# First phase in a fixed order with batched modulation, and mixers with 32-column products gathered

## The chip, the cores and the metric

The kernel runs on one core of one Trainium2 chip. The metric is device time in microseconds, as the median of several runs. One further execution was profiled; times "at" some microsecond below count from the start of its span.

## The reference, cut to what matters

One layer (DEPTH 1) is applied to 256 prompt rows and to 8 single-row samples that carry a recurrent state. All products with weights are in float32 accuracy.

```python
mod = silu(c) @ w_ada + b_ada                  # 2048 x 12288, six parts
h = rmsnorm(x, g_pre_mix) * (1 + sc1) + sh1
z = h @ w_in                                   # 2048 x 15376
y_a = spatial gating of gelu(z_uv)             # branch A
y_b = HGRN2 recurrence, 8 heads, 128 x 128     # branch B, state S' = f S + k v^T
y_c = GLA recurrence, 4 heads, 128 x 256       # branch C, the same form
merged = sum over n of sigmoid(z_gate[n]) * (y_n @ w_branch[n])
x = x + gt1 * rmsnorm(merged @ w_out, g_post_mix)
x = x + gt2 * rmsnorm(relu(h2 @ w_mlp_up)**2 @ w_mlp_down, g_post_mlp)
```

Outputs are the rows of prompt and samples, the final states of both recurrences, and branch A's normalised v rows of the samples.

## The kernel before, in words

**Layout.** Features lie on partitions, 16 feature tiles of 128. The columns are the 256 prompt rows and the 8 samples, 264 in all. The weights are the stationary operand. Each weight block is split into two float32r parts (`split`: ACT casts the high part, L102, and DVE subtracts for the low part, L99), and so are the activations; a product of a 128x128 weight tile is three matmuls of 264 columns (L459, L460, L461 in `granule`). There are 13872 of these matmuls, and they are what the kernel is about.

**Stream of weights.** `plan` lists every block of weights in the order of use. `Stream` loads a block of 512 KB over SP (L419) three blocks ahead of its use and splits it two blocks ahead. A block feeds 24 matmuls and is called an item below. Raw blocks have 6 buffers (`raw`), the split halves 4 (`whi`, `wlo`), which is two items.

**Modulation.** `mod` is needed before `h`. Its products put the 9 conditioning vectors on 32 columns of the PE array, and four such products with their own column strip fill 128 columns (`ada_step`, L236; `ada_round`, L265). The trace shows two records for each of these float32 products. The shift and scale of the first sub-layer are computed by `ada_first` for two or four feature tiles at a time (CHUNKS 2, 2, 4, 4, 4), while the first phase multiplies the feature tiles that are already known with the first 5120 columns of w_in. `ada_round` computes the other parts later, one step of four products at a time.

**Stages.** After a start (x loaded, normed, transposed; first chunk of the modulation) come the first phase (1920 matmuls), the GLA columns (816), branch A with its gates (1152), the gate tiles of branch B (384), branch B (1152), gate tiles of C (384), branch C (1152), the output projection (768) and the MLP (6144). The stages from the GLA columns to branch C are called the mixers' stages here: beside their matmuls run, as generators, `mixer_a`, three `mixer_r` (two groups of HGRN2 heads, one of GLA heads) and, for each group, `samples_r`.

**Generators and queues.** `linear` calls `granule` and then lets three queues advance by fixed rates: `bg` (the mixers), `bs` (the samples), `ba` (rounds of the modulation). That fixes the program's order. The order on each engine is then decided by the framework's scheduler, which models the engines and transfers and may move an instruction ahead of others where its operands allow it.

**Samples.** `samples_r` makes 8 steps for each HGRN2 group and 16 for GLA. A step fetches 256 KB of state (`st`, 3 buffers, L777) and 256 KB of broadcast values (`vbc`, 2 buffers, L779, from a scratch in device memory), both over SP, two steps ahead in the program. ACT scales the state (L791), DVE adds (L793), Pool writes it back (L794), and PE reads it out on 32-column strips (L799). Buffer `st` is free for the next fetch only after that read-out.

**Small products on 32 columns.** Beside L236, L265 and L799 there are the levels of the recurrences' decay matrices: `small_level` (L852, 32 products of 32 columns) and the halves of 32 (L908, 16 products on 32 columns) and of 64 (L916, 8 products on 64 columns).

Of the kernel before, what the change touches and what calls it, by code (L numbers as in the profile page):

```python
# [35 lines left out]
RATES = ((1.7, 0.2, 0.3), (1.5, 0.35, 0.32), (1.5, 0.25, 0.28), (1.0, 0.05, 0.22))  # L36
ST_BUFS = 3
# [3 lines left out]
NQ = 28.0  # L41
R0 = 0.34
ADA_AHEAD = 1
# [3 lines left out]
FILL = (5.0, 9.0)  # L47


@with_exitstack  # L50
def hybrid_step_kernel(
# [53 lines left out]
    # ---------------------------------------------------------------- constants  # L105
    cst = const([P, 904], "cst")
    nc.sync.dma_start(cst, consts)
# [3 lines left out]
    nc.gpsimd.dma_start(msk, masks.rearrange("p (l t) -> p l t", l=6))  # L111

    # ---------------------------------------------------------------- small vectors
# [7 lines left out]
    # x: prompt rows as two token tiles, the samples' feature tiles as rows  # L121
# [8 lines left out]
    nc.sync.dma_start(st1[0:96, :], flat128(b_ada))  # L130
    nc.sync.dma_start(st1[96:112, :], flat128(g_pre_mix))
    nc.sync.dma_start(st1[112:128, :], flat128(g_post_mix))
# [3 lines left out]
    for v, n in rows2:  # L136
        nc.gpsimd.dma_start(st2[n2:n2 + n, :], flat128(v))
        n2 += n

# [7 lines left out]
    ps = sm()  # L147
    T.transpose(ps[:, 0:128], st1, ident)
    T.transpose(ps[:, 128:128 + n2], st2[0:n2, :], ident[0:n2, 0:n2])
    vec = const([P, 128 + n2], "vec")  # L150
    V.tensor_copy(vec, ps[:, 0:128 + n2])
    V.tensor_scalar(vec[:, 172:175], vec[:, 172:175], 0.5, None, ALU.mult)
# [22 lines left out]
    def sum_features(v, n, w):  # L175
        """Sums of v [P, n, w], which it overwrites, over its features (partitions and n tiles), on every partition."""
        while n > 1:
            n //= 2
            add(v[:, 0:n, :], v[:, 0:n, :], v[:, n:2 * n, :])
        ps = sm([P, w])  # L180
# [1115 lines left out]
```

## Time and profile before

| | us |
|---|---|
| runs, median of 3 (lowest to highest) | 2010.1 (2008.6 to 2014.9) |
| profiled execution, span | 2009.9 |
| PE busy / PE weight loads / DVE / ACT / POOL in that span | 1948.6 / 1814.9 / 1191.6 / 1002.0 / 40.5 |
| mean granted PE clock | 0.988 |
| HBM traffic over the span | 219 GB/s |

The profiled execution has no time of its own beside its span; the span stands 0.2 us below the median of the runs, and sums below are made against it. PE matmuls are pipelined, so that a mean duration of 288 ns does not mean one matmul each 288 ns: what counts is the pitch from start to start. A row of the timeline gives start, length, engine, line, operation, tiles and count; in brackets stands the idle time before it and what ended that. "x8" on a line of the modulation is eight records, that is, four products.

### The profile page before, as it was taken

The numbers are of one execution on the slowest core, as the hardware profiler recorded it, in microseconds if no ns is written. First come the engines' busy times: TensorE is split into PE (matmuls) and PEld (weight loads), VectorE is DVE, ScalarE is ACT, GpSimd is POOL, SyncE is SP. The second block draws the span as 40 slices with busy tenths as digits, with TensorE's granted clock in tenths as the row PEclk, the third lists the DMA queues.
The fourth block names the chain that finished last, engine by engine and source line by source line (L and its number), as shares of the span: only waits on it lengthen the run. The fifth ranks groups of instructions, "written<-read, shape, count | busy, mean of one in ns | idle before, by whom it ended". The sixth has DMA issues, their size and how long they took to land.

```text
span 2009.9 us, 42161 instructions
## 1 busy us (share of the span) xinstructions
PE 1948.6 (97%) x17020; PEld 1814.9 (90%) x17020; DVE 1191.6 (59%) x2105; ACT 1002.0 (50%) x1773; POOL 40.5 (2%) x66
## 2 busy tenths in 40 slices
PE   5999999999999999899899999999999999999997
PEld 4779898989988987789899995999999999999996
DVE  3456566777475687445555556555555555555656
ACT  4434354576664574454444445555444445454543
POOL 1000000000000000000000000000000000000000
PEclk9999999999999999999999999999999999999998
DMA  9887978787798668887555866655555555555552
GB/s 311 289 300 244 292 229 250 219 276 222 255 286 280 211 207 255 271 273 228 189 179 180 271 200 231 212 185 179 180 183 182 181 179 184 179 183 180 180 179 84
DMA packets 378179, 442.05 MB, mean 220 GB/s; under 512 B 14914, under 2 KB 339136, under 8 KB 377984
## 3 DMA queue, kind: packets, MB, share of 16 engines
q1 hardware_dynamic: 372592, 424.27, 66.7%
q0 software_dynamic: 4496, 13.90, 1.9%
q8 instruction: 133, 2.18, 0.4%
q10 hardware_dynamic: 896, 1.19, 0.2%
q14 instruction: 62, 0.51, 0.1%
HBM read 427.60 MB, written 11.70 MB: 219 GB/s over the span
## 4 chain that ended last, share of the span: by engine, by line
PE 91%; DMA 4%; DVE 2%; ACT 2%; issue 1%; SPq 0%; ACTq 0%; DVEq 0%
PE mm L459 28%; PE mm L460 27%; PE mm L461 27%; PE ada L265 3%; DMA st<-in_state_gla_dram 2%; PE ada L236 2%; DMA raw<-in_w_ada_dram 1%; PE sm L540 1%; PE sm L799 1%; DVE wlo L99 1%; ACT whi L102 1%; DMA raw<-in_w_in_dram 1%; PE sm L852 1%; DMA st<-in_state_hgrn_dram 0%; DMA b<-in_g_post_mix_dram 0%
## 5 line engine op out<-in xcount | busy, mean ns | idle before, releaser
L459 PE MATMUL mm<-b,whi 128*128 128x264 f32 x4624 | 1332.1, 288 | 17.3 <-ACT b L102 8.0
L460 PE MATMUL mm<-b,whi 128*128 128x264 f32 x4624 | 1321.9, 286 | 1.5 <-DVE b L99 1.5
L461 PE MATMUL mm<-b,wlo 128*128 128x264 f32 x4624 | 1317.3, 285 | 3.2 <-DVE wlo L99 3.2
L99 DVE TENSOR_TENSOR wlo<-raw,whi 128x512 fp32r<-128x512 f32 x1156 | 790.6, 690 | 654.1 <-ACT whi L102 616.3
L102 ACT CAST whi<-raw 128x512 fp32r<-128x512 f32 x1156 | 709.1, 619 | 799.5 <-PE mm L460 720.8
L459 PEld LDWEIGHTS mm<-b,whi 128*128 128x128 f32 x4624 | 873.4, 189 | 78.6 <-issue 31.4
L461 PEld LDWEIGHTS mm<-b,wlo 128*128 128x128 f32 x4624 | 872.8, 189 | 13.4 <-issue 7.2
L460 PEld LDWEIGHTS mm<-b,whi 128*128 128x128 f32 x4624 | 873.4, 189 | 11.4 <-issue 8.8
L96 DVE TENSOR_TENSOR b<-b,mm 128x528 f32<-128x528 f32 x136 | 94.9, 698 | 17.8 <-PE mm L461 17.7
L265 PE MATMUL ada<-raw,cT 128*32 128x512 f32 x464 | 75.6, 616 | 3.0 <-DMA raw<-in_w_ada_dram 3.0
L791 ACT ACTIVATE st<-st,fs 128x128 f32<-128x128 f32 (+1 forms) x96 | 37.0, 430 | 69.9 <-DMA st<-in_state_gla_dram 46.3
L793 DVE SCALAR_TENSOR_TENSOR st<-vbc,b,st 128x128 f32<-128x128 f32 (+1 forms) x96 | 33.9, 390 | 62.1 <-ACT st L791 49.0
L236 PE MATMUL ada<-raw,cT 128*32 128x256 f32 (+1 forms) x640 | 43.9, 359 | 3.0 <-DMA raw<-in_w_ada_dram 3.0
L93 DVE TENSOR_TENSOR b<-b,b 128x512 f32<-128x512 f32 (+1 forms) x47 | 33.7, 739 | 2.0 <-ACT b L869 1.6
L794 POOL DMA_DIRECT2D out_dram<-st x32 | 23.5, 736 | 411.0 <-DVE st L793 381.8
L236 PEld LDWEIGHTS ada<-raw,cT 128*32 128x32 f32 x640 | 14.8, 113 | 13.5 <-DMA raw<-in_w_ada_dram 3.7
L265 PEld LDWEIGHTS ada<-raw,cT 128*32 128x32 f32 x464 | 12.2, 110 | 15.7 <-DMA raw<-in_w_ada_dram 6.6
L99 DVE TENSOR_TENSOR b<-gt,b 128x528 fp32r<-128x528 f32 x32 | 22.6, 708 | 3.2
L93 DVE TENSOR_TENSOR gt<-vt 128x528 f32<-128x528 f32 x32 | 22.4, 700 | 0.0
L99 DVE TENSOR_TENSOR b<-b 128x1024 f32<-128x1024 f32 (+1 forms) x21 | 22.3, 1064 | 0.1
L1202 ACT ACTIVATE b<-vt 128x528 fp32r<-128x528 f32 x32 | 20.7, 647 | 1.0
L1196 ACT ACTIVATE vt<-mm 128x528 f32<-128x528 f32 x32 | 19.4, 607 | 0.0
(284 smaller groups left out, 729.5 us busy)
## 6 DMA issues: line engine op xcount, KB each, us to landing
raw<-in_w_in_dram SPq DMA_DIRECT2D x242, 512.0 KB, 5.3
raw<-in_w_ada_dram SPq DMA_DIRECT2D x164, 512.0 KB, 5.2
raw<-in_w_mlp_up_dram SPq DMA_DIRECT2D x128, 512.0 KB, 3.8
raw<-in_w_mlp_down_dram SPq DMA_DIRECT2D x128, 512.0 KB, 3.6
raw<-in_w_branch_dram SPq DMA_DIRECT2D x48, 512.0 KB, 5.1
raw<-in_w_out_dram SPq DMA_DIRECT2D x32, 512.0 KB, 4.3
raw<-in_w_ada_dram SPq DMA_DIRECT2D x32, 256.0 KB, 5.6
vbc<-vs_d SPq DMA_DIRECT2D x32, 256.0 KB, 6.7
```

The lines of the kernel that those rows point to most:

```text
L93: V.tensor_tensor(o, a, b, op=ALU.mult)
L96: V.tensor_tensor(o, a, b, op=ALU.add)
L99: V.tensor_tensor(o, a, b, op=ALU.subtract)
L102: S.copy(hi, src)
L236: T.matmul(acc[32 * j:32 * j + 32, 0:n], cT[:, k, :], w[:, n * j:n * j + n], start=k == 0, stop=k == KT - 1)
L265: T.matmul(acc[32 * j:32 * j + 32, :], cT[:, k, :], ws[j // 2][:, j % 2 * 512:j % 2 * 512 + 512], start=k == 0, stop=k == KT - 1)
L459: T.matmul(o, a, xh(k + j), start=first and j == 0, stop=False)
L460: T.matmul(o, a, xl(k + j), start=False, stop=False)
L461: T.matmul(o, b, xh(k + j), start=False, stop=last and j == n - 1)
L791: S.activation(st[:, i, :], st[:, i, :], AF.Copy, scale=fs[:, h0 + i, b:b + 1])
L793: V.scalar_tensor_tensor(st[:, i, :], v[:, i, :], k[:, h0 + i, NP + b:NP + b + 1], st[:, i, :], ALU.mult, ALU.add)
L794: nc.gpsimd.dma_start(G.s_out(b, h0, nh), st)
```

## The change: what it does

**First phase.** `manual_schedule` fixes the order on PE, SP and Pool to the program's order. `ada_first` becomes the class `First`: its weights go to the general `blk` buffers instead of the 6 raw ones, their loads are emitted early in a chunk (`paced`), and four blocks' products are issued together (ADA_BATCH). For the first chunk the order of loads and products is written out: six blocks of w_ada, the first block of w_in, the last two of w_ada. The small vectors, most of the constants and the masks are loaded on other queues or later; branch A's four constant tiles are loaded in the last chunk over SP instead of at the start over Pool. The transposes of x for feature tiles 4 to 15 move from the start into the first six granules. For chunks of four tiles two neighbouring blocks of w_in are loaded as rows of 512 columns (PAIRED).

**Mixers.** The order on PE and Pool is fixed to the program's order. Generators mark their narrow products with `yield NARROW` and some wide ones with `yield READY`; a marked generator is held at least until the next granule, and `background` issues the waiting narrow products of `bg` and `bs` together with a step of the modulation. The read-outs of the GLA samples are made for four heads at once. The two halves' products (L908, L916) become full-width ones (L1047, 8 products of 128x64 for either half). State and value fetches go to Pool's queue (L910, L912), with 4 `st` buffers. The rates of the queues are higher. `parts()` comes before the first gate product of a branch.

Output projection and MLP keep their code and their order by the scheduler.

```diff
-RATES = ((1.7, 0.2, 0.3), (1.5, 0.35, 0.32), (1.5, 0.25, 0.28), (1.0, 0.05, 0.22))
-ST_BUFS = 3
+RATES = ((1.8, 0.35, 0.36), (1.7, 0.45, 0.36), (1.6, 0.4, 0.36), (1.0, 0.4, 0.36))
+ST_BUFS = 4
+ADA_BATCH = 4
+ADA_LEAD = 3
+    order = tc.manual_schedule(engines={mybir.EngineType.PE, mybir.EngineType.SP, mybir.EngineType.Pool})
+    order.__enter__()
...
+        def load(self, b):
+            w = blk([P, self.kn, 2, self.n * P])
...
+                nc.sync.dma_start(w[:, i], w1[k * P:(k + 1) * P, :, self.k0 * P:(self.k0 + self.n) * P])
...
+        def paced(self, count):
+            end = count - (5 if count > 9 else 1) - ADA_LEAD
+            at = [b * end // self.nb for b in range(self.nb)]
...
+                if at[b0 + ADA_BATCH - 1] + ADA_LEAD <= g:
+                    for b in range(b0, b0 + ADA_BATCH):
+                        self.steps(b)
+                    b0 += ADA_BATCH
...
+    def background():
+        now[0] += 1
+        bg.pump(rate[0])
+        bs.pump(rate[1])
+        ba.owed = min(ba.owed + rate[2], SLOT_LATE) if ba.g else 0.0
+        held = [q for q in (bg, bs) if q.open(NARROW)]
+        if ba.owed >= SLOT_LATE or held and (not ba.g or ba.owed >= 0.0 or now[0] - min(q.at for q in held) >= SLOT_WAIT):
+            bg.slot()
+            bs.slot()
+            if ba.owed >= 0.0 and ba.g:
+                ba.step()
...
+    for b in range(6):
+        first.load(b)
+    stream[0].load(0)
+    for b in (6, 7):
+        first.load(b)
...
+            if ci == 0 and 2 * gi + 4 < KT:
+                x_transposed(2 * gi + 4)
...
             st = tmp([P, nh, dv], "st", ST_BUFS)
-            nc.sync.dma_start(st, G.s_in(b, h, nh))
+            nc.gpsimd.dma_start(st, G.s_in(b, h, nh))
             v = tmp([P, 4, P], "vbc", VB_BUFS)
-            nc.sync.dma_start(v, vs_d[G.i, h * nj:h * nj + 4, b, :].partition_broadcast(P))
+            nc.gpsimd.dma_start(v, vs_d[G.i, h * nj:h * nj + 4, b, :].partition_broadcast(P))
...
+            if h0 + nh < 4:
+                continue
+            yield NARROW
             ps = sm([P, dv])
-            for i in range(nh):
-                h = h0 + i
-                T.matmul(ps[32 * h:32 * h + 32, :], qm[:, h, b, :], st[:, i, :], start=True, stop=True)
+            for h in range(4):
+                T.matmul(ps[32 * h:32 * h + 32, :], qm[:, h, b, :], sts[h // nh][:, h % nh, :], start=True, stop=True)
...
+            for h in range(4):
+                for hf in range(2):
+                    b = e[:, h, P * hf:P * hf + P]
+                    rhs = b.rearrange("p (n j) -> p n j", j=2 * m)[:, :, m:2 * m]
+                    T.matmul(ps[:, 2 * h + hf, :].rearrange("p (n j) -> p n j", j=m), b, rhs, start=True, stop=True)
```

How the order moves on PE in the first phase (`ada` is the accumulator of the modulation, `mm` that of the streamed product). Before, in the first chunk's granules, two of the small runs of L236:

```order
L459 MATMUL mm_544<-b_330,whi_400 128x264
L236 MATMUL ada_408<-raw_483,cT 32x128 x4
L460 MATMUL mm_544<-b_331,whi_400 128x264
L461 MATMUL mm_544<-b_330,wlo_401 128x264
L459 MATMUL mm_544<-b_330,whi_396 128x264
L460 MATMUL mm_544<-b_331,whi_396 128x264
L236 MATMUL ada_408<-raw_483,cT 32x128 x4
L461 MATMUL mm_544<-b_330,wlo_397 128x264
```

In the changed kernel, in the second chunk's granules, one batch (L256 is the same product):

```order
L534 MATMUL mm_1000<-b_297,wlo_884 128x264
L256 MATMUL ada_852<-b_891,cT 32x256 x4
L256 MATMUL ada_852<-b_893,cT 32x256 x4
L256 MATMUL ada_852<-b_895,cT 32x256 x4
L256 MATMUL ada_852<-b_897,cT 32x256 x4
L532 MATMUL mm_1053<-b_297,whi_933 128x264
L533 MATMUL mm_1053<-b_298,whi_933 128x264
```

From the first L459 (L532) of the first phase to its last matmul, PE's order has 62 stretches of L236 before and 14 stretches of L256 now, with the same number of products; those of L265 (L286) stay at 6.

PE in branch B, beside the GLA samples (`sm` is a small PSUM tile). Before, a read-out, a level and a step of the modulation stand each by itself, 24 matmuls apart:

```order
L461 MATMUL mm_9783<-b_2689,wlo_9813 128x264
L799 MATMUL sm_9983<-st_9600,b_9325 32x256 x2
L459 MATMUL mm_9989<-b_9051,whi_9846 128x264
...
L461 MATMUL mm_9989<-b_9051,wlo_9851 128x264
L852 MATMUL sm_10026<-b_9928 32x32 x32
L459 MATMUL mm_9989<-b_9055,whi_9917 128x264
...
L461 MATMUL mm_9989<-b_9055,wlo_9922 128x264
L265 MATMUL ada_8946<-raw_9939,cT 32x512 x2
L265 MATMUL ada_8946<-raw_9945,cT 32x512 x2
L459 MATMUL mm_10113<-b_330,whi_9971 128x264
```

Now the three follow one another, and the read-out covers two state tiles:

```order
L534 MATMUL mm_9283<-b_2032,wlo_9225 128x264
L987 MATMUL sm_9402<-b_9319 32x32 x32
L936 MATMUL sm_9435<-st_9027,b_9025 32x256 x2
L936 MATMUL sm_9435<-st_9155,b_9025 32x256 x2
L286 MATMUL ada_8743<-raw_9277,cT 32x512 x2
L286 MATMUL ada_8743<-raw_9279,cT 32x512 x2
L532 MATMUL mm_9283<-b_2869,whi_9308 128x264
```

Over the mixers' stages the stretches of products on 32 or 64 columns go from 89 to 48.

Pool's queue in the first HGRN2 group. Before it holds the write-backs only:

```order
L794 DMA out_dram<-st_4967 128x4x128
L794 DMA out_dram<-st_5239 128x4x128
L794 DMA out_dram<-st_5498 128x4x128
L794 DMA out_dram<-st_5666 128x4x128
L794 DMA out_dram<-st_5841 128x4x128
```

Now each fetch stands in one fixed line with them:

```order
L910 DMA st_5594<-in_state_hgrn_dram 128x4x128
L912 DMA vbc_5596<-vs_d 128x4x128
L928 DMA out_dram<-st_5208 128x4x128
L910 DMA st_5753<-in_state_hgrn_dram 128x4x128
L912 DMA vbc_5755<-vs_d 128x4x128
L928 DMA out_dram<-st_5414 128x4x128
```

The fetch of `st_5594` takes the buffer of `st_4928`, the first of this group, and `vbc_5596` is queued behind it. On ACT and DVE, whose order is still the scheduler's, two to three items of casts and subtractions stand between the read-out that frees such a buffer and the scaling and addition that use its new content (before: two to four).

More of the change, by code (lines that the diff above doesn't have):

```diff
@@ L138, in hybrid_step_kernel @@
         n2 += n
+    nc.gpsimd.dma_start(cst[:, 256:904], consts[:, 256:904])
+    nc.gpsimd.dma_start(msk, masks.rearrange("p (l t) -> p l t", l=6))
     ps = sm()
@@ L220, in hybrid_step_kernel, with x_transposed @@
     norm_rows(xt, xsT, xsn, rx)
-    scale_rows(xt, rx)
-    xT = [blk() for _ in range(4)]
-    for k in range(0, KT, 2):
+    xT = []
+    def x_transposed(k):
+        if k % 4 == 0:
+            xT.append(blk())
         ps = transposed(xt, k)
@@ L509, in hybrid_step_kernel, with const_a @@
         ba.g.append(ada_round(r))
-    run(ada_first(0, CHUNKS[0]))
+    consts_a = []
+    def const_a(src):
+        consts_a.append(blk([P, 8, P]))
+        nc.sync.dma_start(consts_a[-1], src)
+    srcs_a = [
+        sgu_ln_g[0].partition_broadcast(P).rearrange("p (g n) -> p g n", g=8),
+        sgu_ln_b[0].partition_broadcast(P).rearrange("p (g n) -> p g n", g=8),
+        sgu_w_s[0].rearrange("g n m -> n g m"),
+        sgu_b_s[0].rearrange("g n -> (g n)").partition_broadcast(P).rearrange("p (g n) -> p g n", g=8),
+    ]
+    stream.append(Stream(plan()))
+    first = First(0, CHUNKS[0])
+    for b in range(6):
[3 more added lines that the diff above has]
+        first.load(b)
+    for i in (1, 2):
+        stream[0].load(i)
+    for b in range(4):
+        first.steps(b)
+    scale_rows(xt, rx)
+    x_transposed(0)
+    x_transposed(2)
+    for b in (4, 5):
+        first.steps(b)
+    small_vectors()
+    for b in (6, 7):
+        first.steps(b)
+    first.sums()
+    first.rows()
     k0 = 0
@@ L513, in hybrid_step_kernel @@
         final = ci == len(CHUNKS) - 1
-        nq = Queue()
+        gn = 4 // n
+        ng = len(begin) // gn
         if not final:
-            nq.g.append(ada_first(k0 + n, CHUNKS[ci + 1]))
-        gn = 4 // n
-        for gi in range(0, len(begin), gn):
+            nxt = First(k0 + n, CHUNKS[ci + 1]).paced(ng)
+        for gi in range(ng):
             accs = [new_acc() for _ in range(gn)]
-            granule(win, 0, n, begin[gi][0], gn * CW, accs, hH, hL, k0, True, True)
-            for acc, (c0, dst, fn) in zip(accs, begin[gi:gi + gn]):
+            granule(win, 0, n, begin[gi * gn][0], gn * CW, accs, hH, hL, k0, True, True)
+            for acc, (c0, dst, fn) in zip(accs, begin[gi * gn:gi * gn + gn]):
                 z = acc[:, :, 0:NT]
@@ L528, in hybrid_step_kernel @@
                     S.activation(dst, dst, fn)
-            if final:
+            if ci == 0 and 2 * gi + 4 < KT:
+                x_transposed(2 * gi + 4)
+            if not final:
+                next(nxt, None)
+            else:
                 ba.pump(rate[2])
-            nq.pump(NQ * gn / 18)
-        nq.drain()
+                if gi % 3 == 0 and srcs_a:
+                    const_a(srcs_a.pop(0))
+        if not final:
+            run(nxt)
         k0 += n
+    order.__exit__(None, None, None)
     def to_tokens(vt):
@@ L646, in mixer_a @@
             yield
+    order = tc.manual_schedule(engines={mybir.EngineType.PE, mybir.EngineType.Pool})
+    order.__enter__()
     gen_a = mixer_a()
@@ L740, in gla_group @@
         z = zin(9216, P)
-        lr = tmp([16, NT], "lr", 1)
         S.copy(lr, z[0:16, 0, :])
-        for m in range(4):
-            ps = sm()
-            T.matmul(ps[:, 0:NT], wup[:, m * P:(m + 1) * P], lr, start=True, stop=True)
-            V.tensor_scalar(G.g[:, m, :], ps[:, 0:NT], bupT[:, m:m + 1], None, ALU.add)
         for s in range(4):
@@ L749, in gla_group @@
             S.copy(pair(G.v[s // 2], s % 2), z)
+            ps = sm()
+            T.matmul(ps[:, 0:NT], wup[:, s * P:(s + 1) * P], lr, start=True, stop=True)
+            V.tensor_scalar(G.g[:, s, :], ps[:, 0:NT], bupT[:, s:s + 1], None, ALU.add)
         G.s_in = lambda b, h, n: state_gla[0, b, h:h + n].rearrange("h k v -> k h v")
@@ L1100, in hybrid_step_kernel @@
     branch(2, lambda: parts_c(gates_c))
+    order.__exit__(None, None, None)
     ba.drain()
```

293 lines of the change are left out of this document (166 added, 127 removed).

## The prediction

> **What bounds the kernel now.** I read the page's busy times and its chain first, to see which engine sets the end.
>
> ```profile
> PE 1948.6 (97%) x17020; PEld 1814.9 (90%) x17020; DVE 1191.6 (59%) x2105; ACT 1002.0 (50%) x1773; POOL 40.5 (2%) x66
> PE 91%; DMA 4%; DVE 2%; ACT 2%; issue 1%; SPq 0%; ACTq 0%; DVEq 0%
> ```
>
> PE is both the busiest engine and the chain. A busy PE need not be at its best pitch, so the next view is the busy time by stage: start, first phase, mixers' stages, and a calm piece of the MLP as the measure.
>
> ```profile
> 0.00:33.50 33.50, 13.34 (x168) 9.41 (x168) 11.27 (x48) 15.56 (x27) 9.05 (x20) 0.99 0.97 317
> 33.50:329.10 295.60, 291.53 (x2487) 252.73 (x2488) 165.35 (x285) 127.45 (x211) 0.00 (x0) 0.99 0.84 272
> 329.10:1108.40 779.30, 758.53 (x7188) 692.35 (x7187) 491.25 (x906) 424.76 (x812) 31.47 (x46) 0.98 0.74 235
> 1300.00:1400.00 100.00, 100.00 (x827) 100.00 (x826) 54.55 (x80) 52.76 (x88) 0.00 (x0) 1.00 0.58 182
> ```
>
> The last row gives the pitch of the streamed matmuls: 100 us / 827 = 0.121 us. The first phase has 1920 of them, 232 us of its 295.6; 63 us go elsewhere. The mixers' stages have 5040, 610 us of 779.3; 169 us go elsewhere. Little of this is idle PE (4.1 and 20.8 us): most is what stands between the streamed matmuls. These 63 + 169 us, and the 33.5 us of the start, are all that the change can touch.
>
> **What a small product costs.** The timeline of PE around one run of L236 on 128 columns, and around one on 256:
>
> ```profile
> 42.68 0.28 PE L459 MATMUL mm<-b,whi 128*128 128x264 f32 x1
> 42.90 0.43 PE L236 MATMUL ada<-raw,cT 128*32 128x128 f32 x8
> 43.25 0.39 PE L460 MATMUL mm<-b,whi 128*128 128x264 f32 x1
> 43.48 0.29 PE L461 MATMUL mm<-b,wlo 128*128 128x264 f32 x1
> ```
>
> ```profile
> 131.52 0.29 PE L460 MATMUL mm<-b,whi 128*128 128x264 f32 x1
> 131.74 0.64 PE L236 MATMUL ada<-raw,cT 128*32 128x256 f32 x8
> 132.31 0.39 PE L461 MATMUL mm<-b,wlo 128*128 128x264 f32 x1
> 132.54 0.28 PE L459 MATMUL mm<-b,whi 128*128 128x264 f32 x1
> ```
>
> From 42.68 to 43.48 there would be two pitches, 0.24; the four products cost 0.56. From 131.52 to 132.54 they cost 0.78. Double columns add 0.22, so that 0.22 and 0.44 is work and 0.34 us is the price of going to the narrow form and back. That price is per stretch, and the stretch is what the change makes rarer.
>
> **First phase.** L236 falls from 62 stretches to 14 with the same products: 48 x 0.34 = **-16.3 us**. PE has nothing beside it that hides this. The other waits of PE in the phase, after the first matmul:
>
> ```profile
> PE ada L236 <- DMA raw<-in_w_ada_dram: 1.9, 2, 1.2
> PE mm L459 <- DVE b L96: 0.9, 1, 0.9
> PE mm L461 <- DVE wlo L99: 0.7, 1, 0.7
> ```
>
> The modulation's loads now have their own buffers and three granules of lead, about 9 us at 24 matmuls each. I take **-3 us** of these 3.5, with bounds 0 and -3.5 and a rival below for the other side.
>
> **Start.** The chain in order of time shows what the first matmul waited for, and the timeline what the transposes cost.
>
> ```profile
> 20.89 11.43 DMA raw<-in_w_in_dram
> ...
> 33.54 0.81 PE mm L459 x2
> ```
>
> ```profile
> 20.53 1.53 PE L206 MATMUL sm<-cst,b 128*128 128x128 f32 x12 [1.03 <-ACT b L211]
> ```
>
> The first block of w_in was asked for at 20.89, behind all of w_ada's first blocks, and landed at 32.32. Now it stands ahead of the last two of them, and branch A's constants (four tiles of 512 KB, 2.1 MB) leave the start. At the 317 GB/s of the start 2.1 MB are 6.6 us. The last block of w_ada then ends the wait, and the chain from it over sums, transposes and modulation to the first split remains, so I take **-4 us** between 0 and -6.6. Twelve transposes take (1.53 - 0.28) / 11 = 0.11 us each; 24 of them leave the start, where PE waited anyway, and come to lie between matmuls: 24 x 0.11 and six returns of 0.1 are **+3.3 us**. The sum up to the GLA columns is -20.0.
>
> **Mixers, work on PE.** The narrow stretches fall from 89 to 48: 41 x 0.34 = **-13.9 us**. Two works change. For the halves the rows are these: the old form on 64 columns (L916), and as the nearest full-width one L935.
>
> ```profile
> 497.21 0.28 PE L461 MATMUL mm<-b,wlo 128*128 128x264 f32 x1
> 497.42 1.15 PE L916 MATMUL sm<-b 128*64 128x64 f32 x16
> 498.50 0.39 PE L459 MATMUL mm<-b,whi 128*128 128x264 f32 x1
> 498.72 0.28 PE L460 MATMUL mm<-b,whi 128*128 128x264 f32 x1
> ```
>
> ```profile
> 505.72 0.29 PE L461 MATMUL mm<-b,wlo 128*128 128x264 f32 x1
> 505.84 1.05 PE L935 MATMUL sm<-b,b 128*128 128x128 f32 x8
> 506.65 0.37 PE L459 MATMUL mm<-b,whi 128*128 128x264 f32 x1
> 506.86 0.28 PE L460 MATMUL mm<-b,whi 128*128 128x264 f32 x1
> ```
>
> Less two pitches, L916 cost 1.27 for eight products, 0.93 without the stretch's price, 0.12 each; L935 cost 0.90 for four, 0.22 each. The 48 new products of L1047 lie between 5.8 and 10.6 us, nearer to L935, since they load full-width weights too. L916 gave up 3 x 0.93 = 2.8, and L908 between nothing and as much again. The balance is between +0.2 and +7.8; I take **+6**. The GLA read-outs, two products in a run before, fill all four column strips now:
>
> ```profile
> 777.30 0.62 PE L799 MATMUL sm<-st,b 128*32 128x256 f32 x4
> 777.85 0.39 PE L459 MATMUL mm<-b,whi 128*128 128x264 f32 x1
> ```
>
> Two products took 0.55 inside a stretch, and four of that width 0.44 in L236; eight runs fewer are between 0 and -4.4, and I take **-3**. The work comes to -10.9.
>
> **Mixers, waits.** Two of the waits of PE there, the stretches at half clock, and the waits of ACT for states:
>
> ```profile
> PE mm L459 <- ACT whi L102: 7.9, 4, 3.6
> PE sm L950 <- ACT b L943: 3.7, 1, 3.7
> ```
>
> ```profile
> sum 23.70, PE 18.98 PEld 14.63 DVE 14.19 ACT 10.47 POOL 3.82; mean PE 4.74 PEld 3.66 DVE 3.55 ACT 2.62 POOL 0.96
> ```
>
> ```profile
> ACT st L791 <- DMA st<-in_state_gla_dram: 46.3, 12, 7.9
> ACT st L791 <- DMA st<-in_state_hgrn_dram: 21.0, 7, 6.2
> ```
>
> Idle PE is 20.8 us (window row). The second fence is the sum over four windows, from 650.8, 790.8, 852.2 and 975.1, in which the granted clock was 0.50; 19.0 busy us at half clock lose 9.5. Together 30 us. Their main cause is the third fence: a state tile is fetched when PE's read-out frees its buffer, ACT reaches the scaling before it has landed, and the casts of the weights queue behind. PE sees only the longest: where ACT waited 7.9 and 6.2, PE waited 3.7 and 3.6, so the split halves in hand cover some 3.4 us.
>
> The change keeps this chain. 20 fetches (4, 4 and 12) still wait for a buffer, now freed by 14 read-outs. What differs is the queue:
>
> ```profile
> vbc<-vs_d SPq DMA_DIRECT2D x32, 256.0 KB, 6.7
> L794 POOL DMA_DIRECT2D out_dram<-st x32: 707/736/809, 414.0 to 928.7; - x32
> DMA to landing us min/median/max: 4.8/6.7/9.3
> ```
>
> (The last row is that of `vbc`.) Before, `vbc` was asked for well ahead of the release; now it stands on Pool behind the fetch that waits for it. Pool's issue takes 0.74 us, so `vbc` lands about 0.74 + 6.7 = 7.4 us after the release, at most 10.0. DVE comes to it two to three items of casts later, less the 1.25 items by which the four split halves let the casts lead: 1.25 x 2.9 = 3.6 us. It waits 3.8, of which 3.4 are covered. A release costs PE 0.4 at the median and 3.0 at the longest; I take 1.2, 17 us over 14. Four places in the new order ask for a fourth small PSUM tile where there are three; with PE held for a copy of about 1 us each that is 5 us. So 30 become 22, **-8 us**; what hid behind the old waits is late next by nothing I can see, since the streamed loads stay on SP.
>
> The Trainium skill speaks against this move: "DMA: Bandwidth & Descriptors", section "Latency and other measured facts", has the first byte of Pool's DMAs, which software describes, at about 1 us against 0.6 for SP's; by it the fetches come 0.4 us later and the sum would be 14 x 0.4 = 5.6 us worse. The trace agrees in direction by Pool's 0.74 us an issue.
>
> **Sum.** -20.0 - 10.9 - 8 = -38.9; 2009.9 - 38.9 = 1971.0, and the median of the runs is 0.2 above the span: **1971 us**. Output projection and MLP keep their 901.5 us.
>
> **Rivals.** (a) *The waits nearly vanish*: four `st` buffers and held read-outs give time, and only the 5 us of PSUM stay; with a start at its bound, -17 - 2.6 gives 1951. For it: ACT waited 12 + 7 times for states, and PE only 4 times for the casts of L102. Against it: two items are less than before. (b) *The loads come in a burst*: in the second chunk `paced` emits 16 blocks of 512 KB in two granules on SP, ahead of the streamed blocks. 8.4 MB at 317 GB/s are 26.5 us; three items ahead and two granules cover 14.5. If nothing had been loaded earlier, PE waits 12 us: 1983. Against it: SP runs ahead wherever buffers are free. (c) *Slower: Pool's one line holds the samples back.* Without the 17 us the sum is 1954; it passes 2010 when a release costs 4.0 us, that is, when the data lands 3.6 + 3.4 + 4.0 = 11.0 us after it. At 12 us it is 1954 + 14 x 5 = 2024. The rows end at 10.0, so I hold it unlikely. The Trainium skill's "SBUF — State Buffer", section "SBUF: two separate sides", gives a way to it (descriptors of Pool's DMAs wait while DVE holds the shared port); the 809 ns maximum of L794 shows no such wait so far. (d) *Gathering saves nothing*, because the 0.34 us belongs to a block of weights and not to a stretch: 16.3 + 13.9 come back, 2001. Against it: both widths give the same fixed part.
>
> **How the numbers follow.** 0.3% (6 us) is about what a measurement of this kernel can tell from no change. My forecast has 0.52 and spans 1957 to 1985 by the bounds above (PSUM and releases 5 to 36, halves, start); (a) 0.24; (b) 0.12; (c) 0.06; (d) 0.06, half of it within 0.3% of before. Faster 0.91, the same 0.03, slower 0.06. The range 1945 to 2000 holds the forecast, (a) and (b), and leaves (c) and (d) out.
>
> **What would show it.** Right: stretches of L256 of 16 or 32 products with one gap of about 0.34 beyond their work; first matmul near 29.5; first phase over by about 309; PE idle in the mixers near 20 us, with ACT or DVE waiting on `st` or `vbc` before it. Wrong: long waits of PE on w_ada between the third and the seventh granule of the second chunk (b); `vbc` landing 11 us or more after the read-out (c); a fixed part in every block of L256 (d).

## The result, and the profile after

The changed kernel takes 2024.1 us (median; 2020.3 to 2029.0), beside 2009.4 us for the kernel before in the same series. The ratio is 1.0065, with a 95% interval of 1.0041 to 1.0089: slower, where 1971 us were forecast. The profiled execution took 2021.9 us, its span is 2020.1 us.

The page of the changed kernel, the busy times and then the chain:

```profile
PE 1932.8 (96%) x16972; PEld 1821.0 (90%) x16972; DVE 1183.6 (59%) x2097; ACT 1000.8 (50%) x1773; POOL 85.8 (4%) x128
PE 74%; issue 12%; DMA 5%; DVE 1%; POOL 1%; ACT 1%; DVEq 0%; POOLq 0%; ACTq 0%
```

PE is busy 15.8 us less than before and the span is 10.2 us longer: 26 us of idle PE have come in. The chain shows it too: 74% of it is PE's, against 91% before, and 12% is "issue", time of an engine for which the profile shows no wait. The busy times by stage (start, first phase, mixers' stages, the rest) say where:

```profile
0.00:29.30 29.30, 12.13 (x144) 6.03 (x144) 11.03 (x47) 15.01 (x26) 6.48 (x16) 0.97 0.95 322
29.30:312.50 283.20, 277.99 (x2512) 257.11 (x2513) 164.49 (x287) 127.26 (x212) 0.52 (x1) 0.98 0.84 285
312.50:1118.80 806.30, 759.75 (x7141) 698.11 (x7140) 484.36 (x899) 424.56 (x812) 78.85 (x111) 0.98 0.78 228
1118.80:2020.10 901.30, 882.95 (x7181) 859.78 (x7179) 523.73 (x867) 433.94 (x724) 0.00 (x0) 0.99 0.60 186
```

Start and first phase gain 4.2 and 12.4 us. The mixers' stages go from 779.3 to 806.3, a loss of 27.0; the rest is as it was (901.5). In the mixers idle PE rose from 20.8 to 46.5 us, and the busy time did not fall (758.5 to 759.8). The waits of PE in that stretch, and those of the other engines for a sample's data (us in total, times, longest):

```profile
PE mm L534 <- DVE wlo L104: 28.1, 22, 4.1
PE ada L286 <- DMA raw<-in_w_ada_dram: 12.3, 7, 4.9
PE mm L532 <- ACT whi L107: 4.7, 5, 2.2
...
ACT st L925 <- DMA st<-in_state_gla_dram: 36.8, 12, 5.8
ACT st L925 <- DMA st<-in_state_hgrn_dram: 35.0, 8, 8.1
DVE st L927 <- DMA vbc<-vs_d: 73.9, 17, 9.6
...
POOL st L910 <- PE sm L936: 169.7, 12, 41.4
```

PE waits for split weights; the engines that split them wait for states and values: 72 us on ACT (L925, 67 before) and now 74 us on DVE too (L927). The 12.3 us on w_ada (0.3 before) nobody had foreseen: the loads of the modulation's next step are asked for when raw buffers come free, and these come free when DVE has split. At these loads SP waits 161.8 us for DVE in the mixers' stages, 89.5 before.

How the mixers' loss divides, as lengths in us from the first streamed matmul of a stage to that of the next:

| | GLA columns | A | gates B | B | gates C | C | sum |
|---|---|---|---|---|---|---|---|
| before | 126.9 | 178.0 | 68.5 | 203.0 | 53.4 | 149.6 | 779.3 |
| changed | 135.7 | 205.8 | 61.9 | 216.3 | 46.8 | 139.7 | 806.3 |

The three stages with nearly all samples beside them lose 50 us; the others give back 23. In the gate columns PE has fewer products than before (532 and 388 records in place of 621 and 431); in C it has as many, and the 6.1 us of idle time and the stretch at half clock there are gone.

### The profile page after: what moved, and what is told of

Its sections match the earlier page's. It is cut to its first block, busy times and chain, and to the rows that moved or that the text cites. A ratio compares the mean times of both kernels' runs of the same rounds, so it can differ in the third digit from the quotient of the medians.

```text
span 2020.1 us, 42073 instructions
## 1 busy us (share of the span) xinstructions
PE 1932.8 (96%) x16972; PEld 1821.0 (90%) x16972; DVE 1183.6 (59%) x2097; ACT 1000.8 (50%) x1773; POOL 85.8 (4%) x128
## 3 DMA queue, kind: packets, MB, share of 16 engines
q1 hardware_dynamic: 330880, 409.19, 64.3%
## 4 chain that ended last, share of the span: by engine, by line
PE 74%; issue 12%; DMA 5%; DVE 1%; POOL 1%; ACT 1%; DVEq 0%; POOLq 0%; ACTq 0%
PE mm L532 23%; PE mm L533 23%; PE mm L534 23%; DMA out_dram<-st 2%; PE ada L286 2%; DMA vbc<-vs_d 2%; PE ada L256 1%; PE sm L663 1%; POOL st L910 0%; PE sm L1047 0%; DMA st<-in_state_gla_dram 0%; DVE wlo L104 0%; POOL vbc L912 0%; DVE b L1377 0%; DMA vs_d<-sqs 0%
## 5 line engine op out<-in xcount | busy, mean ns | idle before, releaser
L532 PE MATMUL mm<-b,whi 128*128 128x264 f32 x4624 | 1331.3, 288 | 10.9 <-ACT whi L107 4.7
L532 PEld LDWEIGHTS mm<-b,whi 128*128 128x128 f32 x4624 | 875.4, 189 | 65.4 <-ACT whi L107 24.0
L286 PE MATMUL ada<-raw,cT 128*32 128x512 f32 x464 | 74.7, 607 | 15.7 <-DMA raw<-in_w_ada_dram 15.7
L927 DVE SCALAR_TENSOR_TENSOR st<-vbc,b,st 128x128 f32<-128x128 f32 (+1 forms) x96 | 34.5, 392 | 87.5 <-DMA vbc<-vs_d 73.9
L925 ACT ACTIVATE st<-st,fs 128x128 f32<-128x128 f32 (+1 forms) x96 | 37.2, 430 | 82.7 <-DMA st<-in_state_gla_dram 36.8
L256 PE MATMUL ada<-b,cT 128*32 128x256 f32 (+1 forms) x640 | 35.1, 354 | 9.5 <-ACT b L207 6.7
L286 PEld LDWEIGHTS ada<-raw,cT 128*32 128x32 f32 x464 | 13.1, 109 | 29.6 <-DMA raw<-in_w_ada_dram 22.8
L256 PEld LDWEIGHTS ada<-b,cT 128*32 128x32 f32 x640 | 17.7, 112 | 22.2 <-DMA b<-in_w_ada_dram 6.9
L912 POOL DMA_DIRECT2D vbc<-vs_d x32 | 24.1, 754 | 70.2 <-DVE st L927 44.2
```

What stands on the lines that cost most here:

```text
L256: T.matmul(acc[32 * j:32 * j + 32, 0:n], cT[:, k, :], w[:, n * j:n * j + n], start=k == 0, stop=k == KT - 1)
L286: T.matmul(acc[32 * j:32 * j + 32, :], cT[:, k, :], ws[j // 2][:, j % 2 * 512:j % 2 * 512 + 512], start=k == 0, stop=k == KT - 1)
L532: T.matmul(o, a, xh(k + j), start=first and j == 0, stop=False)
L912: nc.gpsimd.dma_start(v, vs_d[G.i, h * nj:h * nj + 4, b, :].partition_broadcast(P))
L925: S.activation(st[:, i, :], st[:, i, :], AF.Copy, scale=fs[:, h0 + i, b:b + 1])
L927: V.scalar_tensor_tensor(st[:, i, :], v[:, i, :], k[:, h0 + i, NP + b:NP + b + 1], st[:, i, :], ALU.mult, ALU.add)
```

## The experiments

Each time is the median of its runs, and the ratio is to the kernel before on the same chip. Run names: e1 to e18.

| run | first phase | fetches | read-outs, halves | order on PE | rates | us | ratio (95% interval) |
|---|---|---|---|---|---|---|---|
| changed | new | Pool | gathered | fixed | new | 2024.1 | 1.0065 (1.0041 to 1.0089) |
| e4 | new | SP | as before | scheduler | before | 1990.8 | 0.9913 (0.9896 to 0.9929) |
| e10 | new | Pool | as before | scheduler | before | 2018.4 | 1.0046 (1.0032 to 1.0060) |
| e13 | new | st on Pool | as before | scheduler | before | 2006.5 | 0.9985 (0.9968 to 1.0001) |
| e14 | new | vbc on Pool | as before | scheduler | before | 1998.2 | 0.9935 (0.9912 to 0.9958) |
| e16 | new | SP | as before, 4 st | scheduler | before | 1993.4 | 0.9914 (0.9894 to 0.9935) |
| e15 | new | SP | read-outs gathered, 4 st | scheduler | before | 2002.2 | 0.9965 (0.9948 to 0.9981) |
| e12 | new | SP | both gathered, 4 st | scheduler | before | 2005.1 | 0.9984 (0.9972 to 0.9996) |
| e17 | new | SP | as before, held | scheduler | mixed | 1990.8 | 0.9911 (0.9895 to 0.9926) |
| e18 | new | SP | as before, held | fixed | mixed | 1999.3 | 0.9941 (0.9920 to 0.9961) |
| e11 | new | SP | gathered, held | scheduler | mixed | 1995.2 | 0.9929 (0.9915 to 0.9943) |
| e9 | new | SP | gathered, held | fixed | mixed | 2001.5 | 0.9967 (0.9956 to 0.9979) |
| e6 | new | SP | gathered, held | fixed | before | 2001.4 | 0.9958 (0.9941 to 0.9975) |
| e8 | new | SP | gathered, held | fixed | new, modulation before | 2010.1 | 1.0002 (0.9993 to 1.0010) |
| e1 | new | SP | gathered, held | fixed | new | 2010.5 | 1.0009 (0.9998 to 1.0020) |
| e2 | new | vbc on SP | gathered, held | fixed | new | 2014.3 | 1.0020 (1.0005 to 1.0035) |
| e5 | new | Pool | gathered, held | fixed | before | 2038.1 | 1.0139 (1.0121 to 1.0157) |
| e3 | new | Pool | gathered, held | Pool free | new | 2034.5 | 1.0127 (1.0110 to 1.0145) |
| e7 | new | Pool | gathered, read-outs READY | fixed | new | 2024.5 | 1.0064 (1.0045 to 1.0082) |

### First round: which half, and which queue

e1 puts both fetches back on SP, e2 only `vbc`:

```diff
-            nc.gpsimd.dma_start(st, G.s_in(b, h, nh))
+            nc.sync.dma_start(st, G.s_in(b, h, nh))
...
-            nc.gpsimd.dma_start(v, vs_d[G.i, h * nj:h * nj + 4, b, :].partition_broadcast(P))
+            nc.sync.dma_start(v, vs_d[G.i, h * nj:h * nj + 4, b, :].partition_broadcast(P))
```

> The changed kernel with both fetches of a state step (st and vbc) issued by SyncE again instead of Pool. Pool-line theory (a fetch that waits in Pool's line for a gathered read-out makes the data late, VectorE waits for vbc 74 us, the splits come late and TensorE waits 28 us for them): TensorE's 28.1 us on wlo fall under 8 us and about 10 us of half clock behind them go, mixers near 775 us, time 1990 to 1998 us. Release rival (the buffers themselves come free late, because one read-out for eight products frees two or four of them; whichever queue asks, it waits as long, and on SyncE the weight loads stand behind it): 2015 to 2030 us. Modulation rival (the late w_ada loads and the held order are the loss): about 2018 us.

> The changed kernel with only the vbc fetch on SyncE; st stays on Pool. Pool-line theory in its narrow form (vbc, whose own buffer is long free, stands behind a st fetch that waits): VectorE's 74 us on vbc fall under 20 us, but ScalarE still waits for st (72 us), TensorE's waits about halve, time 2003 to 2012 us. If the wait for st alone carries the loss: 2018 to 2026 us, as the changed kernel. If vbc was all of it: 1990 to 1998 us, as with both moved.

e3 takes Pool out of the fixed order in the mixers:

```diff
-    order = tc.manual_schedule(engines={mybir.EngineType.PE, mybir.EngineType.Pool})
+    order = tc.manual_schedule(engines={mybir.EngineType.PE})
```

> The changed kernel with Pool's order in the mixers left to the scheduler; TensorE's stays fixed, the fetches stay on Pool. If Pool's fixed line is the loss (a ready transfer behind a waiting one): 1992 to 2005 us. If the buffers' release is the loss, whatever the line: within 6 us of the changed kernel's 2024 us.

e4 keeps the changed first phase and takes the mixers of the kernel before (their code from `to_tokens` to the last `branch`, its `Queue`, rates and three state buffers; only branch A's constants still come in the first phase).

> The first phase of the changed kernel, with the mixers of the kernel before (their order, rates, buffers, narrow work and SyncE fetches as before). All theories: the first phase ends 16 to 17 us sooner and nothing takes it back, 1991 to 1996 us. If the earlier end is given back (the modulation's or side loads' work pushed into the mixers): 2000 to 2010 us.

e4 came out at 1990.8: the first phase's gain is real and is not given back, and the mixers' 779.2 us are those of before. So all of the loss lies in the mixers' part of the change. e1 recovered 13.7 us of 33 (by the ratios 11 of 31, since the runs are from different chips). Its waits of PE:

```profile
PE mm L534 <- DVE wlo L104: 11.4, 11, 4.9
PE mm L532 <- ACT whi L107: 10.8, 6, 5.9
PE ada L286 <- DMA raw<-in_w_ada_dram: 6.7, 7, 2.8
PE sm L1088 <- ACT b L1091: 6.3, 1, 6.3
```

The waits on `wlo` fell by 17 us as the Pool-line theory had it, but more were left than it allows, and those on `whi` grew; the other 20 us had to be something else. e2 took most of the same gain. e3 went the wrong way: the scheduler's order on Pool, with the fetches there, is 10 us worse than the fixed one. So Pool's *fixed* line is not the fault, against what my theory said.

### Second round: rates and release

e5 and e6 take the rates of before, with the fetches on Pool and on SP; e8 takes back the modulation's rate alone, on SP:

```diff
-RATES = ((1.8, 0.35, 0.36), (1.7, 0.45, 0.36), (1.6, 0.4, 0.36), (1.0, 0.4, 0.36))
+RATES = ((1.7, 0.2, 0.3), (1.5, 0.35, 0.32), (1.5, 0.25, 0.28), (1.0, 0.05, 0.22))
```

> The changed kernel with the rates of the kernel before (samples 0.2/0.35/0.25/0.05 and modulation 0.3/0.32/0.28/0.22 a granule for 0.35/0.45/0.4/0.4 and 0.36); fetches on Pool, order held. Rates theory (the higher rates pack state and w_ada loads and the VectorE and ScalarE steps into the GLA columns and the first two branches, where the DMA engines are busy 0.81 to 0.89 of the time): waits there fall by half, mixers near 790 us, 2005 to 2012 us. Pool-line theory alone (the rates cost nothing): 2020 to 2028 us.

> Both fetches on SyncE and the rates of the kernel before: what is left of the change in the mixers is the fixed order and the gathering. If line and rates are the whole loss: mixers near 775 to 780 us, 1986 to 1994 us. If the held order or the gathering itself costs: 2000 us or more. If the rates don't matter: 2010 us, as with the fetches alone moved.

> Both fetches on SyncE and only the modulation's rates of the kernel before (0.3/0.32/0.28/0.22 for 0.36). Modulation theory (its 1 MB a step crowds the DMA engines and its own late loads stop TensorE for 6.7 us): 2001 to 2006 us. If only the samples' rates matter: 2008 to 2012 us.

e7 releases a gathered read-out as soon as its data can be there:

```diff
-            yield NARROW
+            yield READY
             ps = sm([P, dv])
```

> The changed kernel with the gathered read-outs released as soon as their data can be there, not held for a slot among the narrow work; fetches on Pool. Release theory (the read-out held back frees the state buffers late, and Pool's fetch waits 170 us for that): Pool's wait for the read-out falls by half or more and 8 to 14 us of the loss go, 2010 to 2016 us, less some 4 us for the turn to narrow work that each read-out then pays alone (0.34 us times 12 or so). Pool-queue theory (the queue makes the landing late, not the release): 2022 to 2030 us.

The rates theory failed with the fetches on Pool (e5, 14 us slower) and held in sign on SP (e6, 9 us faster). In both the gate columns of B grow from 62 us to 89.6 and 84.4: PE waits there for the last steps of a recurrence (6.1 us at L1133) and for the read-out of samples left over (4.1 us at L1146). Why the other stages give back more than that on SP and less on Pool is not shown. e8 left nothing to the modulation's rate; with e9 below, which differs from e8 in the samples' rates alone and runs 8.6 us sooner (7 by the ratios), those 9 us are the samples' rates. e7 changed nothing: holding the read-out for a slot costs nothing.

### Third round: what each part does on the mixers of before

e9 is e1 with the rates of before for samples and modulation, and those of the change for the recurrences (1.8, 1.7, 1.6, 1.0; "mixed" in the table). e11 is e9 without `manual_schedule` in the mixers. e10 is e4 with both fetches on `nc.gpsimd`. e12 is e4 with four state buffers, the read-outs of GLA made for four heads at once and the halves as in the changed kernel:

```diff
-ST_BUFS = 3
+ST_BUFS = 4
...
+            sts.append(st)
             yield 0.5
+            if h0 + nh < 4:
+                continue
             ps = sm([P, dv])
...
+            for h in range(4):
+                T.matmul(ps[32 * h:32 * h + 32, :], qm[:, h, b, :], sts[h // nh][:, h % nh, :], start=True, stop=True)
```

> Both fetches on SyncE, the rates of the kernel before for samples and modulation, the changed kernel's higher rates for the recurrence (1.8/1.7/1.6/1.0). Drain theory (what was left with all rates of before, 10 us over the first phase alone, is the recurrence that held steps make late, drained at once ahead of branch 1 where the gate columns took 84.4 us against 67.8): the gate columns fall to about 66 us, 1984 to 1992 us. Order theory (the fixed order of TensorE costs by itself): 1997 us or more.

> The changed first phase with the mixers of before, and only the two fetches of a state step moved to Pool, in the scheduler's order. Queue theory (Pool as the queue of the fetches costs by itself, the stores and waits of its line ahead of each fetch): 2003 to 2012 us. Order theory (it costs only where the line is fixed or the read-outs are held): 1990 to 1997 us.

> Both fetches on SyncE, mixed rates, holds and gathering as changed, but the order of TensorE and Pool in the mixers left to the scheduler. If the fixed order of TensorE is worth something once the fetches are on SyncE: 3 to 10 us slower than with the order fixed. If it is nothing: within 2 us of it.

> The changed first phase with the mixers of before (scheduler's order, SyncE fetches, rates of before), and of the mixers' change only the gathered read-outs with four state buffers and the halves as eight products of 128 rows. Work theory, by the prediction's terms (gathered GLA read-outs -3, halves +6): 1991 to 1996 us, 0 to +5 against the first phase alone. Release rival (the shared read-out frees buffers late even so): 1997 us or more.

e9: the drain theory fell. The gate columns of B did fall from 84.4 us (e6) to 64.3, but branch A took back 16 of these 20 us and the other stages the rest; the time stayed at 2001.5. e11: the fixed order is no gain, it costs 6 us. e12 fell into the rival's range. The clearest is e10: the two fetches alone, in the scheduler's order, cost 27.6 us, of which the profiled executions show 21.5 in the mixers' stages (that of e4 was the slowest of its six, 1996.4 us). Mixers' stages, waits, and times from issue to landing (last column, us) of e4 and then of e10:

```profile
313.90:1093.10 779.20, 756.72 (x7188) 689.78 (x7187) 490.89 (x906) 423.87 (x813) 31.40 (x46) 0.99 0.76 235
```

```profile
ACT st L894 <- DMA st<-in_state_gla_dram: 45.5, 12, 7.9
...
ACT st L894 <- DMA st<-in_state_hgrn_dram: 26.4, 8, 6.4
...
PE mm L526 <- ACT whi L107: 8.9, 3, 3.7
```

```profile
q0 software_dynamic: 3584, 11.64, 3.8%
...
vbc<-vs_d SPq DMA_DIRECT2D x32, 256.0 KB, 7.0
...
st<-in_state_gla_dram SPq DMA_DIRECT2D x16, 256.0 KB, 5.7
st<-in_state_hgrn_dram SPq DMA_DIRECT2D x13, 256.0 KB, 4.8
```

```profile
316.40:1117.10 800.70, 765.34 (x7188) 694.66 (x7187) 489.60 (x906) 422.80 (x813) 76.60 (x107) 0.98 0.77 229
```

```profile
ACT st L894 <- DMA st<-in_state_gla_dram: 61.9, 11, 8.5
...
ACT st L894 <- DMA st<-in_state_hgrn_dram: 34.5, 8, 8.1
...
PE mm L526 <- ACT whi L107: 22.6, 12, 4.8
```

```profile
q0 software_dynamic: 8464, 27.63, 15.1%
...
vbc<-vs_d POOLq DMA_DIRECT2D x32, 256.0 KB, 7.6
...
st<-in_state_gla_dram POOLq DMA_DIRECT2D x16, 256.0 KB, 7.4
st<-in_state_hgrn_dram POOLq DMA_DIRECT2D x13, 256.0 KB, 5.5
```

The states land 0.7 to 1.7 us later, ACT waits 24 us more for them, and PE waits 12 times for `whi` instead of 3.

### Fourth round: landing or line, read-outs or buffers

e13 has only `st` on Pool, e14 only `vbc`. e16 is e4 with a fourth state buffer (and, as in the changed kernel, four scratch tiles under shared names); e15 is e16 with the read-outs gathered and the halves left as before (the diff of e12 without the halves).

> The changed first phase, the mixers of before, and only the st fetches on Pool (vbc on SyncE). Landing theory (st lands 0.7 to 1.7 us later from Pool and ScalarE waits for it at nearly every step with the weight splits behind): most of the 27 us of both fetches, 2008 to 2018 us. Line theory (st is held up behind a vbc that waits): no vbc in the line, 1991 to 1998 us.

> As above with only the vbc fetches on Pool (st on SyncE). Landing theory: vbc has a lead of 21 us at the median, its later landing costs nothing, 1991 to 1997 us. If vbc on Pool by itself is the cost (Pool's writing of its descriptors, longer transfers that crowd the DMA engines): 2003 us or more. Line theory: 1991 to 1998 us too, since st is on another queue.

> The changed first phase, the mixers of before, four state buffers and only the GLA read-outs gathered, the halves as before. If the halves of 128 rows are the 14 us of the gathering run: 1988 to 1993 us. If the read-outs are: 1999 to 2006 us.

> The changed first phase, the mixers of before, and only a fourth state buffer (the read-outs ungathered). Lead theory (ScalarE's 72 us of waits for st fall when st is asked for a step sooner): 1980 to 1989 us, a kernel faster than both. If the buffer lets the transfers come earlier into a crowded stretch (weights late): 1993 to 2003 us, and then the buffer and not the read-out is what the gathering run lost by.

`st` alone cost 15.6 us (14.5 by the ratios), a little under what the landing theory allowed and far over the line theory. Its waits on ACT and its landings:

```profile
ACT st L894 <- DMA st<-in_state_gla_dram: 53.2, 11, 7.2
...
ACT st L894 <- DMA st<-in_state_hgrn_dram: 42.0, 8, 9.4
...
PE mm L526 <- ACT whi L107: 15.9, 10, 3.4
```

```profile
st<-in_state_gla_dram POOLq DMA_DIRECT2D x16, 256.0 KB, 6.5
...
st<-in_state_hgrn_dram POOLq DMA_DIRECT2D x13, 256.0 KB, 4.9
```

The fetch isn't asked for later. Worked out from the timelines, over the 23 steps that wait for a buffer of their own group, the issue follows the end of the read-out that frees it by 0.1 us at the median on SP (e4; 1.5 on the mean) and by 0.3 us on Pool (e13; 0.7 on the mean). Where ACT waited for `st`, it began 6.3 us after the issue on the mean in e4 (20 steps), 7.1 in e13 (19), 7.2 in e10 (19) and 7.5 in the changed kernel (20). A part of this may be the issue itself, from whose start both count: 0.70 to 0.76 us on Pool in e13, 0.37 to 0.44 at the median on SP in e4. From the read-out to ACT's start it is 7.0 us at the median in e4 and 7.8 in e13, but 7.9 on the mean in both.

So the landing theory has a rival that my expectations left out. With the fetch on another queue the scheduler also ordered ACT and DVE otherwise. In e13 and e10 it put the scaling of `st` one or two casts of weights earlier than in e4 in 11 of the 32 steps (in e14 in 2), and 14.9 of the 23.3 us by which ACT's waits grew from e4 to e13 lie in these 11 steps. A wait ahead of a cast holds that cast up, one behind it does not. No run separates the two: that `st` on Pool costs 15 us is shown, and that its later landing is the reason is argued.

`vbc` alone cost 7.4 us (4.4 by the ratios, with intervals that touch), a little over what the landing theory allowed. Both together cost 8 more by the ratios (27 against 15 + 4); in e10 a `vbc` that waits for DVE's release stands in Pool's line, 228.8 us in all, and that is the place of the line theory, for that remainder. It is argued and not shown.

e15 against e16 sets the read-outs at 8.8 us (10 by the ratios), e12 against e15 the halves at 2.9 (3.8). The fourth buffer alone is within the error of e4; it did not bring the gain that I had put as one theory. In branch B's stage, where GLA's samples run, e15 and then e16:

```profile
690.70:899.90 209.20, 192.90 (x1854) 167.87 (x1853) 123.39 (x221) 113.55 (x229) 13.40 (x19) 0.97 0.80 249
```

```profile
PE mm L526 <- ACT whi L107: 8.0, 3, 3.7
PE sm L1056 <- ACT b L1048: 6.1, 1, 6.1
PE mm L528 <- DVE wlo L104: 2.1, 4, 1.2
```

```profile
688.60:888.90 200.30, 192.93 (x1839) 167.09 (x1837) 124.25 (x223) 113.24 (x227) 12.69 (x18) 0.98 0.80 255
```

```profile
PE mm L526 <- ACT whi L107: 6.0, 4, 3.2
PE mm L528 <- DVE wlo L104: 1.3, 4, 0.6
```

PE is busy for the same 192.9 us and idle for 16.3 instead of 7.4. Over all mixers' stages the work of the runs between the streamed matmuls, without idle time, did fall, by 3.0 us. A shared read-out frees two buffers at once and the first of them later, and the longest wait of ACT for a GLA state in this stage grew from 7.3 to 10.2 us; but the sum of these waits fell, from 34.2 to 27.4. That the later release makes PE idle is therefore argued and not shown.

### Fifth round: is the holding worth anything

e17 keeps of the mixers' change only the marks NARROW and READY with `background`, the mixed rates and four buffers. e18 adds the fixed order of PE and Pool.

> The changed first phase; in the mixers only the held steps (narrow work together, late steps held until ready) and the mixed rates, fetches on SyncE, four buffers, read-outs and halves as before, the scheduler's order. If the parts add up: 1995.2 less 8.8 (read-outs) less 2.9 (halves), 1983 to 1986 us, the fastest of all. If the holds are worth nothing: 1991 to 1995 us, as the first phase alone with three or four buffers.

> The same with the order of TensorE and Pool fixed in the mixers. Order theory (the fixed order costs about 6 us, as 2001.5 against 1995.2): 6 us over the run beside it. If that difference came from the gathered read-outs in the fixed order: within 2 us of it.

e17 is as fast as e4 and no faster: the holds are worth nothing that can be measured in the time (in its profile the mixers' stages are 3.7 us shorter than e4's), and the parts do not simply add up (the sum said 1983 to 1986). e18 is 8.5 us slower (6 by the ratios), so the fixed order costs by itself, about as in e9 against e11. Its idle PE in the mixers' stages is 30.3 us, against 21.3 in e17. The largest waits of PE there (e17, then e18); that the scheduler had put a ready matmul first where the fixed order waits is argued:

```profile
PE mm L532 <- ACT whi L107: 9.7, 5, 3.0
PE mm L534 <- DVE wlo L104: 6.8, 14, 2.7
PE ada L286 <- DMA raw<-in_w_ada_dram: 3.0, 3, 1.8
PE sm L1085 <- ACT b L1088: 1.1, 1, 1.1
```

```profile
PE mm L532 <- ACT whi L107: 14.0, 7, 3.5
PE mm L534 <- DVE wlo L104: 6.2, 16, 2.2
PE sm L983 <- DVE b L98: 5.2, 1, 5.2
PE sm L752 <- DVE srow L748: 2.2, 1, 2.2
```

From e17 to the changed kernel the ratios make one chain: 0.9911, fixed order 0.9941, gathering and new halves 0.9967, the higher rates of samples and modulation 1.0009, fetches on Pool 1.0065. At 2009 us that is +6, +5, +8 and +11 us on top of a first phase that gains 18. The intervals of the first two steps touch. Two other pairs are clear of their errors and show that either costs, though not that it costs as much everywhere: the fixed order 8 us in e9 against e11, gathering and new halves 14 us in e12 against e16. The fastest kernels found are e4 and e17 at 1990.8 us, by the ratios 0.9% under the kernel before and 1.5% under the changed one.

## Why the prediction was wrong, point by point

**First phase: right, but for its waits.** A batch of L256 behaves as forecast. The timeline around one:

```profile
131.35 0.28 PE L534 MATMUL mm<-b,wlo 128*128 128x264 f32 x1
131.56 1.93 PE L256 MATMUL ada<-b,cT 128*32 128x256 f32 x32
133.43 0.39 PE L532 MATMUL mm<-b,whi 128*128 128x264 f32 x1
133.65 0.28 PE L533 MATMUL mm<-b,whi 128*128 128x264 f32 x1
```

From 131.35 to 133.65 there would be two pitches, 0.24; the sixteen products in one stretch cost 2.06, which is also the mean of twelve such batches, where four stretches of four had cost 4 x 0.78 = 3.1. Measured in this way, which is the prediction's, the runs of L236/L256 fell from 45.1 us (without 1.9 of idle time) to 28.8, by the 16.3 that were forecast (two batches with transposes among them are counted at the mean of the other twelve). Rival (d) is out. The start came at 29.3 (near 29.5 was said). The waits failed: idle PE in the phase went from 4.1 to 5.2 us instead of falling by 3, since PE now waits for activations and splits rather than for w_ada; behind two of these waits, at 113.0 us, lies a stretch of 3.4 us at half clock that was not there before. The phase ended at 312.5 where 309 was said: -16.6 against -20.0. Rival (b), the burst, did not show: no wait of PE on w_ada is left in that phase.

**Mixers' work: the term was on the right side and somewhat too large.** Measured as above, over each run between two streamed matmuls and the matmul behind it, less pitches and idle time, the time fell by 7.3 us where 10.9 was forecast. The gathered read-outs saved 3.0 (e15 against e16; -3 taken) and the halves cost 3.7 (e12 against e15; +6 taken, +0.2 to +7.8 as bounds), so that some 8 are left for the 13.9 of the rarer stretches. PE's busy time rose by 1.2 us all the same: the other streamed matmuls took 8.5 us more, 4.7 of them at half clock. And the gathered read-outs brought 9 us of waits, which the prediction had not connected with them.

**Mixers' waits: the step that failed.** The prediction had 30 become 22; idle PE alone is 46.5, and half clock takes 12.9 more, together 59. The 22 were 17 of releases and 5 for PSUM tiles, with nothing for half clock, which had been 9.5 of the 30. Some of its premises held: DVE waits 4.3 us a time, 17 times (3.8 said, 14 times). `vbc` lands 7.9 us after its issue at the median (6.7 taken), and 9.4 us after the read-out, where 7.4 was said. Wrong was above all what this costs. First, ACT's waits were taken to give way to DVE's; they stayed, so that 67 us of waiting became 146, and 14 of DVE's 17 waits lie in steps in which ACT waits too, one behind the other. Second, a cover of 3.4 us was granted at every release, as though the split halves were refilled each time; samples come in groups of steps a few us apart, and I take it that from the second on little is in hand (the halves in hand were not counted). PE waited 27 times for splits, not 14, and 2.3 us per release instead of 1.2. Third, six stretches at half clock lie around or just behind waits of PE of 1.4 to 4.9 us; one of them, and the sum of the six:

```profile
566.90:573.80 6.90, 5.16 (x26) 4.92 (x26) 5.10 (x13) 3.06 (x8) 0.00 (x0) 0.51 0.74 237
...
sum 30.80, PE 25.86 PEld 22.35 DVE 20.08 ACT 12.03 POOL 0.75; mean PE 4.31 PEld 3.73 DVE 3.35 ACT 2.00 POOL 0.12
```

Six windows hold 25.9 busy us, half of them lost, 3.4 more than before. The Trainium skill, "TensorE: Matmul & The Clock Gate", section "What's actually happening", has a gate that halves the clock after an idle window of about 3.4 us; the stretches here are 3.4 and 6.8 us long in the clock's records (cut as 3.4 and 6.9 above), so the length agrees. But a window need not be idle from end to end: in the 3.4 us ahead of the stretch at 399.7 us, PE was busy for 1.5. The 5 us for PSUM tiles did not come up: no wait of PE names one.

**Rival (c) had the right place and sign, and the wrong price.** Slower was given 0.06, on the rule that data must land 11.0 us after the read-out. Over the 20 steps that wait for a buffer of their own group, the fetch of `st` is issued 0.5 us after the read-out at the median (2.2 on the mean, a few are held in the line), and `vbc` lands 9.4 us after it at the median, 11.4 on the mean and 20.2 at the most, where the prediction, from rows of fetches on SP, had 10.0 at the most. So (c)'s condition was met on the mean, and with 11.4 its sum gives 1954 + 14 x 4.4 = 2016. That this comes near 2024 is in part luck: taking both fetches off Pool (e1) gives back 11 us by the ratios, not 62, and Pool's fixed line is not what decides (e3). The rest are costs for which the prediction had no term. The 14.5 to 15.6 us that e13 measured for `st` alone, put into the prediction, would have turned the term of -8 into about +7. The Trainium skill, "DMA: Bandwidth & Descriptors", section "Latency and other measured facts", has first-byte times for the two queues that are 0.4 us apart: the same sign, and the runs show somewhat more, 0.8 us from the issue to ACT's start between e4 and e13.

**Not foreseen.** The prediction had no term for the fixed order of PE (6 to 8.5 us), for the samples' higher rates (7 to 9 us with the fetches on SP), or for late w_ada loads in the mixers (12.3 us of PE's waits).

**What stays open.** Why a state asked for by Pool lands later is not settled; a wait of Pool's issue on DVE, the way that the prediction names under (c), does not show in e13, where no issue of `st` took more than 0.76 us. Nor is it settled how much of `st`'s cost on Pool is the landing and how much the scheduler's other order of ACT, nor why `vbc` and `st` together cost more than each alone.

## What to carry to other kernels

A transfer that an in-order engine waits for at every step has no slack: ask what stands behind the waiting instruction there (here the casts that feed PE), and count a wait at every step and not only at the longest. Take a forecast of a landing from the order in which it will be asked for: here fetches asked for well ahead were made to wait in line, and landed later than any row of before. Where a scheduler orders the engines, moving a transfer to another queue can move its consumers too; compare their order before naming the landing as the cause. And a change of several parts should be measured part by part: here one part gained 18 us and four others lost 30.

## What the runs showed of the hardware that I had not expected

The broadcast fetches (`vbc`) from Pool's queue occupied the DMA engines longer for their bytes. From e4 to e10, q0 took up 16.0 MB more and its share of 16 engines rose from 3.8% to 15.1% of about 800 us. In the packet records `st` and `vbc` run as packets of 512 or 1024 bytes from SP and of 4096 bytes from Pool. Those of `st` are no dearer so: about 201 ns in e13 (183.5 on the mean over 4672 packets of that queue, less the 2816 of the stores at 172, as in e4), where a packet of 1024 bytes from SP, mostly weights, takes 52, so four of them 208. Those of the broadcast `vbc` are: 535 ns in e14, worked out in the same way from 325 over 4864, against 8 x 35 = 280 from SP in e4 (35 on the mean over all packets of 512 bytes there, most of them of `vbc`).
